# A new layout of the first stage of a trunk-layer program: two blocks of x normed together, the first FFN products by k tiles, the modulation's weights stationary

## The chip, the core and the metric

The program runs on one core of a Trainium2 chip. The metric is device time in microseconds (us) of one execution of the whole program; lower is better. An engine here is one of TensorE (PE; its weight loads are listed as PEld), VectorE (DVE), ScalarE (ACT), GpSimd (POOL) and SyncE (SP, which issues nearly all DMAs).

## What is computed

One layer of a hybrid backbone over 128 context tokens and 1024 latent tokens, width 1024, all in float32. The stage that is changed is the beginning of this:

```python
def rms_norm(x, g):
    y = x * rsqrt(mean(x * x) + EPS)
    return y * g
def adaln(cond, mod_w, mod_b):               # 9 vectors of 1024 for each of two conditions
    m = silu(cond) @ mod_w + mod_b           # mod_w is 1024 x 9216
    return m.reshape(-1, 9, 1024)
def swiglu(h, w_in, w_out):
    g, u = split(h @ w_in, 2)                # w_in is 1024 x 5632
    return (silu(g) * u) @ w_out
def trunk_layer(x, mods, ...):
    sh1, sc1, g1, sh2, sc2, g2, sh3, sc3, g3 = mods
    h = rms_norm(x, norm_ffn1) * (1 + sc1) + sh1
    x = x + 0.5 * g1 * swiglu(h, ffn1_w_in, ffn1_w_out)
    ...                                      # mixer (spatial gating MLP, latent attention), FFN 2
```

## The kernel before

**Tiling.** The 1152 tokens are three blocks of 384: block 0 holds the context and two tiles of latent tokens, blocks 1 and 2 only latent tokens. Activations lie transposed, as 8 k tiles of 128 rows (the width) by tokens. FFN 1 takes the blocks in the order 1, 2, 0 and cuts the 1152 columns into two halves of 576, and each half again into two parts (`s` 0 and 1) of 288. Every float32 operand is split into a rounded part and a remainder (`hi`, `lo`), and a product is three matmuls (`mm3`, L169).

**The products of FFN 1.** `seq` lists weight tiles by feature tile f and product number p. The products 1 and 2 of f 0 to 8 are "early": they need only the first half of the columns, p 1 the k tiles 0 to 3 and p 2 the k tiles 4 to 7. There are 18 of them, each of two parts of 12 matmuls, 432 matmuls of 288 columns in all. Their results (`ye`) go to DRAM (`ya_d`) and come back later; `ye` has three buffers, each a pair of two results, and a result with even number takes a new pair. After the early products come the units of the main loop (`units`), one for each f, of seven-product Strassen form. They need the operands of products 3, 5, 6 and 7, which are sums of parts of h; `norm_s` and `sums` (L500 to L505) make them from block 0, the last block, on DVE and ACT.

**Weights.** `make(i)` loads raw weight tiles into a ring of six (`load_parts`), copies them rounded on ACT and takes the remainder on DVE or POOL (`wi`, six buffers).

**The first stage.** `start` runs with ACT, DVE and POOL (and PE, always) in the order in which the code stands; SP is ordered by a scheduler there. It loads block 1 of x, transposes it, loads the modulation's weights for shift 1 and scale 1 (`ch` 0 and 1) in pieces of two k tiles, 1 MB each, and works out 1/rms of block 1. `mod_on_pe` multiplies with the 2-column `s2` stationary and 256 columns of weights moving (L360), copies the two rows out (L363) and transposes them back (L368); one of the eight pieces (scale 6 and 7) goes over ACT and POOL instead (`macs`, L822 and L824, and `sums`, L829). As the pieces come, x times 1/rms (`x_r`), scale and shift with the rounded copy (`h_part`) and the remainder (`l_part`) are made for block 1. Behind it, `x_block(2)` transposes block 2, `up` begins with two parts of early products, and `x_block(0)`, due 3.0 on the recording clock after the start of `up`, transposes block 0 (the clock `clk` counts estimated PE time and sets where such steps are written into the order). PSUM is taken in two layouts: four `ps_up` and four `ps_dn` banks first, then three `ps_two` pairs and two `ps_dn`.

Of the kernel before, what the change touches and what calls it, by code (L numbers as in the profile page):

```python
# [73 lines left out]
def tile_trunk(  # L74
# [15 lines left out]
    def f32(ap):  # L90
        return ap.bitcast(F32)
# [37 lines left out]
    s_ps = ps_pool("ps")  # L129
# [223 lines left out]
    def mod_on_pe(ch, k0, n, w, tp, mid=()):  # L353

        row = tp.tile([2, BW], F32, tag="modrow", name="modrow", bufs=2)
        ps = ps_dn([P, 512])
        for j in range(KT):
            if j in mid:
                mid[j]()
            nc.tensor.matmul(ps[:2, :n * P], lhsT=s2[:, j, :], rhs=w[:, j, :], start=j == 0, stop=j == KT - 1)  # L360
            clk.run(0.21 * n)

        V.tensor_copy(out=row[:, :n * P], in_=ps[:2, :n * P])  # L363

        def end():
            pt = ps_dn([P, n, 2])
            for k in range(n):
                nc.tensor.transpose(pt[:, k, :], row[:, k * P:k * P + P], ident[:2, :2])  # L368
            mod_finish(ch, k0, n, [pt[:, :, cd] for cd in range(2)])
        return end  # L370
# [25 lines left out]
    class Ffn:  # L396
# [5 lines left out]
        def __init__(self, which, order, wi, wo, early, chunks, wseq):  # L402
# [11 lines left out]
            self.ordered = None  # L414
# [160 lines left out]

        def up(self, side):

            add, mult, early, seq, hc, ys, stores = ALU.add, ALU.mult, self.early, self.seq, self.hc, {}, []
            banks = [ps_two() for _ in range(3)]
# [47 lines left out]
            for i0 in range(0, self.n_early, 6):  # L627
                for s in range(2):
                    for i in range(i0, i0 + 6):
                        f, p = seq[i]  # L630
                        self.ready(p, s)
                        ps = banks[f % 3]
                        self.product(ps, self.made[i], hc[p], p == 1, (s,))
                        if i % 2 == 0:
                            pair = self.yt.tile([P, 2, MV], F32, tag="ye", name="ye", bufs=3)
                        y = pair[:, i % 2]
                        S.activation(out=y, in_=ps[:, s, :MV], func=AF.Copy if p == 1 else AF.Silu)
                        dma(self.ya_d[f][:, p - 1, s * MV:s * MV + MV], y)
                        if s == 1:
                            self.make(i + 6)  # L640
# [120 lines left out]
    def big(name):  # L761
        return s_r.tile([P, 3 * D], F32, tag="big", name=name, bufs=3)
# [8 lines left out]
    def transpose_x(b, xn):  # L771

        st = big(f"x{b}").rearrange("p (k t) -> p k t", k=KT)
        r1 = []
        for k in range(KT + 2):
            if k < KT:
                ps = ps_dn([P, BW])
# [8 lines left out]
        dma(x_d[b], st)  # L786
# [9 lines left out]
    def start():  # L796

        m2 = [s_l.tile([P, 2 * KT * P], F32, tag="m", name="modw", bufs=2) for _ in range(2)]
        ml = s_l.tile([P, 3 * D], F32, tag="big", name="modw", bufs=1)
        mq = [F1.tile(f"q{i}", F32, (P, 4 * HT)) for i in range(4)]  # L800
        xn1 = load_x(1, big("xnat1"))
# [3 lines left out]
        sc01 = mod_in(1, 0, mq[0])  # L805
        sh01 = mod_in(0, 0, mq[2])
# [4 lines left out]
        sc67 = mod_in(1, 6, mq[1])  # L811
        sc23 = mod_in(1, 2, mq[3])
        sh23 = mod_in(0, 2, m2[0])
        sc45 = mod_in(1, 4, m2[1])
        sh67 = mod_in(0, 6, ml)
        accs = s_r.tile([P, 2, 256], F32, tag="acc", name="acc", bufs=1)

        def macs(cd):

            for j in range(KT):  # L820
                t = accs[:, cd, :] if j == 0 else t384()[:, 0:256]
                S.activation(out=t, in_=sc67[:, j, :], func=AF.Copy, scale=s2[:, j, cd:cd + 1])  # L822
                if j:
                    G.tensor_tensor(out=accs[:, cd, :], in0=accs[:, cd, :], in1=t, op=ALU.add)  # L824
# [1002 lines left out]
```

## Time and profile before

| | us |
|---|---|
| median of 3 runs | 2924.8 (2924.14 to 2924.87) |
| the profiled execution's own time | 2923.9 |
| its span, first to last instruction | 2922.1 |
| first of block 0's transposes | 61.94 |
| first product of the main loop's first unit | 139.23 |

The profile is of one execution. Lines such as L169 are lines of the kernel before; where a helper records an operation, the line is the helper's. Starts are counted from the span's beginning.

### The profile page before, as it was taken

How to read it: one execution, taken by the hardware profiler on the slowest of the kernel's cores; microseconds unless marked ns; L12 is line 12 of the kernel's file. 1: busy time of each engine (PE TensorE's matmuls, PEld its weight loads, DVE VectorE, ACT ScalarE, POOL GpSimd, SP SyncE). 2: the span in 40 equal slices, each digit the busy share in tenths (PEclk: the TensorE clock that was granted, in tenths of full speed). 3: DMA queues.
4: the chain of work that ended last, by engine and by line, in shares of the span. 5: the costliest groups of instructions: out<-in, count | busy, mean ns of one | idle time of the engine just before them, and what ended most of it. 6: DMA issues, size and time to landing. Idle time of an engine off the chain costs nothing.

```text
span 2922.1 us, 48080 instructions
## 1 busy us (share of the span) xinstructions
PE 2848.2 (97%) x19102; PEld 2812.0 (96%) x19102; DVE 1470.6 (50%) x2874; ACT 980.1 (34%) x2069; POOL 787.4 (27%) x557
## 2 busy tenths in 40 slices
PE   7899999999989999998999999999999999999997
PEld 4899999999989999998999999999999999999997
DVE  5644788888463200248447767734464422233434
ACT  5622333312042311014245555512362233331213
POOL 4156556510010011102322222223016544430000
PEclk9999999999999999999999999999999999999999
DMA  8444444666114122113621111264344422253222
GB/s 297 135 135 144 141 137 145 203 210 209 54 33 147 49 90 90 45 33 98 205 70 44 53 47 34 79 209 146 108 152 132 125 72 80 83 182 103 98 74 101
DMA packets 362453, 335.29 MB, mean 115 GB/s; under 512 B 23204, under 2 KB 320020, under 8 KB 361844
## 3 DMA queue, kind: packets, MB, share of 16 engines
q1 hardware_dynamic: 361556, 330.25, 36.3%
q8 instruction: 150, 2.46, 0.4%
q0 software_dynamic: 672, 1.97, 0.2%
q14 instruction: 75, 0.61, 0.1%
HBM read 242.59 MB, written 83.53 MB: 112 GB/s over the span
## 4 chain that ended last, share of the span: by engine, by line
PE 92%; DVE 4%; ACT 2%; issue 1%; POOL 1%; DMA 0%; SPq 0%; DVEq 0%; ACTq 0%; POOLq 0%
PE ps_two L169 37%; PE ps_up L169 19%; PE ps_dn L169 18%; PE ps_w L169 6%; PE ps_s L169 3%; PE ps_s L1404 2%; PE ps_w L204 2%; PE ps_dn L204 1%; DVE h L151 1%; PE ps_dn L1151 1%; PE ps_dn L360 1%; PE ps_b L169 0%; ACT h L150 0%; ACT q L475 0%; PE ps_dn L242 0%
## 5 line engine op out<-in xcount | busy, mean ns | idle before, releaser
L169 PE MATMUL ps_two<-h,wi 128*128 128x288 f32 x6336 | 862.7, 297 | 12.8 <-DVE wi L151 7.0
L169 PEld LDWEIGHTS ps_two<-h,wi 128*128 128x128 f32 x6336 | 850.6, 189 | 17.1 <-DVE wi L151 8.2
L151 POOL TENSOR_TENSOR wi<-raw,wi 128x512 fp32r<-128x512 f32 (+1 forms) x294 | 448.4, 1531 | 1022.2 <-ACT wi L150 896.0
L150 ACT CAST wi<-raw 128x512 fp32r<-128x512 f32 (+2 forms) x401 | 289.4, 725 | 877.3 <-PE ps_dn L169 291.7
L169 PE MATMUL ps_dn<-h,wi 128*128 128x384 f32 x2256 | 410.8, 339 | 2.6 <-DVE q L620 2.6
L169 PEld LDWEIGHTS ps_dn<-h,wi 128*128 128x128 f32 x2256 | 396.7, 189 | 2.9 <-DVE q L620 2.9
L169 PE MATMUL ps_up<-h_hi,wi 128*128 128x384 f32 x1152 | 302.1, 339 | 0.0
L169 PEld LDWEIGHTS ps_up<-h_hi,wi 128*128 128x128 f32 x1152 | 209.9, 188 | 0.0
L749 DVE SCALAR_TENSOR_TENSOR h<-ps_dn,modG,h 128x128 f32<-128x128 f32 (+2 forms) x205 | 99.3, 508 | 215.6 <-PE ps_dn L169 215.3
L385 DVE SCALAR_TENSOR_TENSOR q<-mraw,s,q 128x512 f32<-128x512 f32 x196 | 194.7, 1033 | 7.7 <-DMA mraw<-in_mod_w_dram 7.7
L169 PE MATMUL ps_up<-h_lo,wi 128*128 128x384 f32 x576 | 194.3, 337 | 0.7 <-DVE h_lo L294 0.7
L1475 POOL TENSOR_SCALAR p<-p,ast 128x1152 f32<-128x1152 f32 x64 | 79.2, 1238 | 303.4 <-PE ps_w L204 107.3
L169 PE MATMUL ps_up<-wi,h_hi 128*128 128x256 f32 (+1 forms) x864 | 160.8, 286 | 0.0
L169 PE MATMUL ps_two<-q,wi 128*128 128x288 f32 x1056 | 146.8, 294 | 0.0
L169 PEld LDWEIGHTS ps_two<-q,wi 128*128 128x128 f32 x1056 | 142.1, 188 | 0.0
L169 PE MATMUL ps_s<-kn,qn 128*128 128x384 f32 x576 | 136.9, 346 | 0.0
L150 ACT CAST pt<-ps_w 128x384 fp32r<-128x384 f32 x192 | 86.9, 488 | 145.6 <-PE ps_w L204 145.5
L169 PEld LDWEIGHTS ps_up<-wi,h_hi 128*128 128x128 f32 x864 | 133.6, 188 | 0.0
L169 PE MATMUL ps_up<-wi,h_lo 128*128 128x256 f32 (+1 forms) x432 | 122.7, 284 | 0.0
L589 ACT ACTIVATE q<-q 128x576 f32<-128x576 f32 x70 | 48.1, 687 | 219.6 <-DVE q L610 147.3
L151 DVE TENSOR_TENSOR wi<-raw,wi 128x512 fp32r<-128x512 f32 (+4 forms) x107 | 101.1, 955 | 38.9 <-ACT wi L150 38.6
L1470 DVE TENSOR_REDUCE ast<-ps_s 128x1 f32<-128x384 f32 x192 | 105.3, 553 | 26.1 <-PE ps_s L1404 24.1
(269 smaller groups left out, 4366.6 us busy)
## 6 DMA issues: line engine op xcount, KB each, us to landing
raw<-in_ffn_w_in_dram SPq DMA_DIRECT2D x212, 256.0 KB, 3.2
mraw<-in_mod_w_dram SPq DMA_DIRECT2D x112, 256.0 KB, 3.7
a_d<-q SPq DMA_DIRECT2D x88, 288.0 KB, 2.3
h<-a_d SPq DMA_DIRECT2D x32, 576.0 KB, 6.2
raw<-in_w_in_dram SPq DMA_DIRECT2D x34, 512.0 KB, 4.2
raw<-in_ffn_w_out_dram SPq DMA_DIRECT2D x32, 448.0 KB, 4.3
ya_d<-ye SPq DMA_DIRECT2D x72, 144.0 KB, 1.8
q<-ya_d SPq DMA_DIRECT2D x36, 288.0 KB, 3.9
```

The lines of the kernel that those rows point to most:

```text
L150: S.copy(out=hi, in_=src)
L151: (lo_eng or G).tensor_tensor(out=lo, in0=src, in1=f32(hi), op=ALU.subtract)
L169: nc.tensor.matmul(ps, lhsT=l[i], rhs=r[j], start=start and i == j, stop=stop and i == 1, skip_group_check=more)
L204: nc.tensor.transpose(out, in_, ident)
L360: nc.tensor.matmul(ps[:2, :n * P], lhsT=s2[:, j, :], rhs=w[:, j, :], start=j == 0, stop=j == KT - 1)
L385: V.scalar_tensor_tensor(out=ac, in0=w, scalar=s2[:, j, cd:cd + 1], in1=ac, op0=ALU.mult, op1=ALU.add)
L589: S.activation(out=y, in_=y, func=AF.Silu)
L749: V.scalar_tensor_tensor(out=xs, in0=ps[:, c0:c1], scalar=modG[:, self.which, cd, dt:dt + 1], in1=xs, op0=ALU.mult, op1=ALU.add)
L1151: nc.tensor.matmul(pm[:, i, :], lhsT=vb[b][:, i, g * P:g * P + P], rhs=wsT[:, g, :], start=True, stop=True)
L1404: nc.tensor.matmul(ps, lhsT=q2[h][:, ts_], rhs=kab[j][:, c0:c1], start=False, stop=j == 1)
L1470: V.reduce_max(out=pts[n][1][:, j:j + 1], in_=ps, axis=AX.X)
L1475: G.tensor_scalar(out=p, in0=p, scalar1=rc, scalar2=0.0, op0=ALU.mult, op1=ALU.add)
```

## The change

- All eight modulation pieces go over PE, with the 128x128 weight tile stationary and the two columns of `s2` moving, so that the result comes out transposed: 16 matmuls a piece in the program, 32 instructions on PE, since each float32 matmul is two. The copy L363, the transposes L368 and the way over ACT and POOL are gone.
- Block 1 and block 2 are both transposed and normed in `start`, with copies out of `ps_dn` and `ps_up` (now `ps_two`) in turn. PSUM has the wide layout from the beginning.
- The products of i 0 to 5 (f 0 to 2, p 1 and 2) move into `start`, part by part as the k tiles' modulation comes (`early_half`), and `up` goes on at i 6.
- The stores of x for blocks 1 and 2 stand late in `start`. SP keeps the written order there too. Block 0's transposes stay at 3.0 on the clock after the start of `up`, so now behind 14 of the 36 early parts, not behind 2.

The rest of the program stays: behind the first units, all engines have the same instructions in the same order.

```diff
-    s_ps = ps_pool("ps")
+    s_ps = ps_pool("ps", wide=True)
...
-            nc.tensor.matmul(ps[:2, :n * P], lhsT=s2[:, j, :], rhs=w[:, j, :], start=j == 0, stop=j == KT - 1)
...
+    def mod_on_pe(ch, k0, n, w):
+
+        ps = ps_dn([P, n, 2])
+        for k in range(n):
+            for j in range(KT):
+                nc.tensor.matmul(ps[:, k, :], lhsT=w[:, j, k * P:k * P + P], rhs=s2[:, j, :], start=j == 0, stop=j == KT - 1)
+        mod_finish(ch, k0, n, [ps[:, :, cd] for cd in range(2)])
...
+        def early_half(self, i, s):
+
+            f, p = self.seq[i]
+            self.ready(p, s)
+            ps = self.banks[f % 3]
+            self.product(ps, self.made[i], self.hc[p], p == 1, (s,))
+            if i % 2 == 0:
+                self.pair = self.yt.tile([P, 2, MV], F32, tag="ye", name="ye", bufs=3)
+            y = self.pair[:, i % 2]
+            S.activation(out=y, in_=ps[:, s, :MV], func=AF.Copy if p == 1 else AF.Silu)
+            dma(self.ya_d[f][:, p - 1, s * MV:s * MV + MV], y)
+            if s == 1:
+                self.make(i + 6)
...
-            for i0 in range(0, self.n_early, 6):
+            for i0 in range(self.begun, self.n_early, 6):
...
+        def m_tile():
+            return s_l.tile([P, 2 * KT * P], F32, tag="m", name="modw", bufs=3)
+        both = (ps_dn, ps_up)
+        xn1, st1, xn2, st2 = big("xnat1"), big("x1"), big("xnat2"), big("x2")
...
+        w[1, 0] = mod_in(1, 0, m_tile())
+        w[0, 0] = mod_in(0, 0, m_tile())
...
+        xn2 = load_x(2, xn2)
+        F1.load_parts(3)
+        w[1, 2] = mod_in(1, 2, m_tile())
+        w[0, 2] = mod_in(0, 2, F1.tile("q1", F32, (P, 4 * HT)))
+        w[1, 4] = mod_in(1, 4, F1.tile("q3", F32, (P, 4 * HT)))
...
+        st1, r1 = transpose_x(1, xn1, st1, both)
...
+        mod_on_pe(1, 0, 2, w[1, 0])
+        mod_on_pe(0, 0, 2, w[0, 0])
+        out1 = norm_rstd(r1)
+        r_1 = out1()
+        w[0, 4] = mod_in(0, 4, m_tile())
+        w[1, 6] = mod_in(1, 6, m_tile())
+        x_r(1, st1, r_1, 0, 0, 1, 2, 3)
+        h_part(1, 0, 0, 1)
+        l_part(1, 0, 1)
+        x_r(1, st1, r_1, 0, 4, 5, 6, 7)
+        st2, r2 = transpose_x(2, xn2, st2, both)
+        F1.take_banks()
+        for i in range(3):
+            F1.make(i, G)
+        mod_on_pe(1, 2, 2, w[1, 2])
+        out2 = norm_rstd(r2)
+        w[0, 6] = mod_in(0, 6, m_tile())
+        F1.load_parts(6)
+        xns[0] = load_x(0, big("xnat0"))
+        mod_on_pe(0, 2, 2, w[0, 2])
+        r_2 = out2()
+        h_part(1, 0, 2, 3)
+        l_part(1, 2, 3)
+        x_r(2, st2, r_2, 0, 0, 1, 2, 3)
+        h_part(2, 0, 0, 1, 2, 3)
+        l_part(2, 0, 1, 2, 3)
+        for i in range(3):
+            F1.early_half(i, 0)
+        mod_on_pe(1, 4, 2, w[1, 4])
+        x_r(2, st2, r_2, 0, 4, 5, 6, 7)
+        mod_on_pe(0, 4, 2, w[0, 4])
+        h_part(1, 0, 4, 5)
...
+        for i in range(3, 6):
+            F1.make(i, G)
+        for i in range(2):
+            F1.early_half(i, 1)
+        mod_on_pe(1, 6, 2, w[1, 6])
+        mod_on_pe(0, 6, 2, w[0, 6])
+        F1.early_half(2, 1)
+        h_part(1, 0, 6, 7)
+        l_part(1, 6, 7)
+        h_part(2, 0, 6, 7)
+        l_part(2, 6, 7)
+        dma(x_d[1], st1)
+        dma(x_d[2], st2)
+        F1.take_x(1)
+        x_r(2, st2, r_2, 1, *range(KT))
+        for s in range(2):
+            for i in range(3, 6):
+                F1.early_half(i, s)
+        h_part(2, 1, *range(KT))
+        F1.begun = 6
...
-    with tc.manual_schedule(engines={mybir.EngineType.Activation, mybir.EngineType.DVE, mybir.EngineType.Pool}):
+    with tc.manual_schedule(engines={mybir.EngineType.Activation, mybir.EngineType.DVE, mybir.EngineType.Pool, mybir.EngineType.SP}):
...
-    x_block(2)
...
-    clk.later(X_FIRST[0], lambda: x_block(0, gap=gap1))
+    clk.later(X_FIRST[0], x_block0)
```

PE at the first modulation pieces. Before, `modw` and `q` hold weights that move through the 2-column `s` (s2), with small transposes of `modrow` between:

```order
L857 MATMUL ps_up<-ident,vec 128x112
L360 MATMUL ps_dn<-q_169,s_114 2x256 x2
L368 MATMUL ps_dn<-ident,modrow 128x2 x2
L360 MATMUL ps_dn<-q_169,s_114 2x256 x6
L360 MATMUL ps_dn<-q_170,s_114 2x256
L204 MATMUL ps_dn<-ident,st 128x128 x3
```

And in the changed program, where `s` moves through the weights:

```order
L204 MATMUL ps_two<-ident,xnat_164 128x128 x3
L846 MATMUL ps_two<-ident,vec 128x112
L358 MATMUL ps_dn<-s_114,modw 128x2 x32
L242 MATMUL ps_dn<-ones,r_221 128x1
L242 MATMUL ps_dn<-ones,r_228 128x1
```

Two whole pieces now stand in one run ahead of block 1's sums of squares (`r`), and `vec` (the gains and mod_b) ahead of both. The counts are those of the program: PE executes each float32 matmul as two instructions.

SP at the stores of x (`x_d_72` is block 1, `x_d_73` block 2, `x_d_71` block 0; `ya_d_137` to `139` are the early results of f 0 to 2). Before:

```order
L88 DMA raw<-in_ffn_w_in_dram 128x4x128 x2
L88 DMA x_d_73<-x_540 128x3072
L88 DMA ya_d_137<-ye 128x288
L88 DMA ya_d_138<-ye 128x288
L88 DMA x_d_71<-x_638 128x3072
L88 DMA ya_d_139<-ye 128x288
```

And now:

```order
L88 DMA raw<-in_ffn_w_in_dram 128x4x128
L88 DMA x_d_72<-x_165 128x3072
L88 DMA x_d_73<-x_167 128x3072
L88 DMA ya_d_137<-ye 128x288
L88 DMA ya_d_138<-ye 128x288
L88 DMA ya_d_139<-ye 128x288
```

Two stores of x, 1.5 MB each, now stand one behind the other ahead of the results of the parts (3,0), (4,0) and (5,0).

ACT at block 0's transposes (`x_638` before, `x_892` now; `t` are squares). Before:

```order
L225 ACTIVATE t_594<-x_540 128x384
L225 ACTIVATE t_597<-x_540 128x384
L225 ACTIVATE t_600<-x_540 128x384
L637 ACTIVATE ye<-ps_two 128x288 x2
L783 COPY x_638<-ps_dn 128x384
L222 ACTIVATE r_654<-x_638 128x384
```

And now (`q_747` and `q_748` are the second half of block 2):

```order
L579 ACTIVATE ye<-ps_two 128x288
L150 CAST wi<-raw 128x512
L834 ACTIVATE q_747<-q_747,modT,modA 128x192 x4
L834 ACTIVATE q_748<-q_748,modT,modA 128x192 x4
L579 ACTIVATE ye<-ps_two 128x288 x2
L782 COPY x_892<-ps_dn 128x384
L222 ACTIVATE r_908<-x_892 128x384
```

Block 0's copies followed block 2's squares; now eight scale-and-shifts of block 2's second half stand between a weight tile of the early products and them.

## Rows read from the trace of the kernel before

**Rows 1.** The page of the profile: the engines' busy time (part 1), TensorE's busy tenths in 40 slices of 73 us (part 2), the chain that ended last by engine (part 4).

```profile
PE 2848.2 (97%) x19102; PEld 2812.0 (96%) x19102; DVE 1470.6 (50%) x2874; ACT 980.1 (34%) x2069; POOL 787.4 (27%) x557
...
PE   7899999999989999998999999999999999999997
...
PE 92%; DVE 4%; ACT 2%; issue 1%; POOL 1%; DMA 0%; SPq 0%; DVEq 0%; ACTq 0%; POOLq 0%
```

**Rows 2.** Windows of 10 us. Columns: the window, its length, busy us (and instructions) of PE, PEld, DVE, ACT and POOL, the granted TensorE clock, the DMA engines' share, GB/s moved.

```profile
10.00:20.00 10.00, 8.99 (x48) 5.32 (x48) 6.78 (x20) 4.30 (x11) 3.19 (x3) 1.00 1.10 342
...
50.00:60.00 10.00, 6.46 (x33) 5.42 (x32) 6.46 (x11) 7.74 (x18) 7.19 (x6) 0.66 0.67 212
...
70.00:80.00 10.00, 7.15 (x51) 6.25 (x49) 6.62 (x32) 4.95 (x14) 0.00 (x0) 0.99 0.32 119
...
100.00:110.00 10.00, 8.58 (x63) 8.11 (x62) 10.00 (x16) 10.00 (x24) 0.00 (x0) 1.00 0.24 79
110.00:120.00 10.00, 6.59 (x43) 6.36 (x42) 10.00 (x16) 8.51 (x18) 0.00 (x0) 0.87 0.30 95
```

**Rows 3.** The timeline of PE. Columns: start in us, length in us, engine, line, operation, out<-in, shapes, count, and idle time before it with its releaser. The first row is the beginning of block 0's transposes, the second begins the first unit of the main loop (four products of 24, in one run), the third the second unit.

```profile
61.94 0.81 PE L204 MATMUL ps_dn<-ident,xnat 128*128 128x128 f32 x6
...
139.23 12.95 PE L169 MATMUL ps_two<-h,wi 128*128 128x288 f32 x96 [0.50 <-ACT ye L637]
...
155.19 12.86 PE L169 MATMUL ps_two<-h,wi 128*128 128x288 f32 x96
```

**Rows 4.** The same timeline of PE, the steps whose prices are used: block 1's transposes (L204), modulation products (L360), the sums of squares (L242), the spreading of 1/rms (L204 of st), the end of block 0's transposes.

```profile
7.43 4.76 PE L204 MATMUL ps_dn<-ident,xnat 128*128 128x128 f32 x22 [1.17 <-DMA xnat<-in_x_sample_dram]
12.13 2.32 PE L360 MATMUL ps_dn<-q,s 128*2 128x256 f32 x10
...
22.98 0.54 PE L204 MATMUL ps_dn<-ident,st 128*128 128x128 f32 x3
...
27.94 3.62 PE L360 MATMUL ps_dn<-modw,s 128*2 128x256 f32 x16
...
65.31 1.03 PE L204 MATMUL ps_dn<-ident,xnat 128*128 128x128 f32 x6 [0.17 <-ACT x L783]
...
67.78 1.39 PE L242 MATMUL ps_dn<-ones,r 128*128 128x1 f32 x12
```

**Rows 5.** The timeline of DVE, ACT and POOL in the first 90 us, the same columns: first and last step of a 1/rms (L247, L213), the copy of its spread (L256), x times it (L865), scale and shift and rounded copy of one k tile (two L840 with the copy L842 between them), remainder (L847), rounded copies of weights (L150), a product's result (L637), the first copy and the last addition of block 0's transposing (L783, L226), eight scale-and-shifts of 192 columns (L475).

```profile
17.15 0.16 DVE L247 TENSOR_SCALAR st<-ps_dn 128x3 f32<-128x3 f32 x1 [1.37 <-PE ps_dn L242]
...
19.11 0.16 DVE L213 SCALAR_TENSOR_TENSOR st<-st 128x3 f32<-128x3 f32 x1
...
23.56 0.48 ACT L256 COPY t<-ps_dn 128x384 f32<-128x384 f32 x1 [9.23 <-PE ps_dn L204]
...
27.32 1.94 DVE L865 TENSOR_TENSOR q<-x,t 128x384 f32<-128x384 f32 x4
...
27.89 0.71 ACT L840 ACTIVATE q<-q,modT,modA 128x384 f32<-128x384 f32 x1 [3.85 <-DVE q L865]
...
29.05 0.70 ACT L840 ACTIVATE q<-q,modT,modA 128x384 f32<-128x384 f32 x1
29.19 0.54 DVE L847 TENSOR_TENSOR h<-q,h 128x384 fp32r<-128x384 f32 x1
...
48.41 2.18 ACT L150 CAST wi<-raw 128x512 fp32r<-128x512 f32 x4
...
60.53 0.41 ACT L637 ACTIVATE ye<-ps_two 128x288 f32<-128x288 f32 x1 [0.31 <-PE ps_two L169]
...
62.46 0.48 ACT L783 COPY x<-ps_dn 128x384 f32<-128x384 f32 x1
...
67.85 1.10 DVE L226 TENSOR_TENSOR r<-r,t 128x384 f32<-128x384 f32 x1 [0.17 <-ACT t L225]
...
82.22 3.62 ACT L475 ACTIVATE q<-q,modT,modA 128x192 f32<-128x192 f32 x8
```

**Rows 6.** The timeline of block 0's norm and of the first unit's weights: the copy of the spread 1/rms, the last four remainders of block 0's operands (DVE), then the first and the last step of the first unit's weights.

```profile
87.00 0.48 ACT L256 COPY t<-ps_dn 128x384 f32<-128x384 f32 x1 [0.37 <-PE ps_dn L204]
...
117.80 2.75 DVE L151 TENSOR_TENSOR q<-q,q 128x576 fp32r<-128x576 f32 x4
...
127.48 0.69 DVE L558 TENSOR_TENSOR s<-raw 128x512 f32<-128x512 f32 x1 [3.91 <-DMA raw<-in_ffn_w_in_dram]
...
131.88 1.29 POOL L151 TENSOR_TENSOR wi<-raw,wi 128x512 fp32r<-128x512 f32 x1 [63.34 <-ACT wi L150]
```

**Rows 7.** DMA issues of the first 140 us. Columns: out<-in, queue, operation, count, KB of one, median us from issue to landing.

```profile
ya_d<-ye SPq DMA_DIRECT2D x36, 144.0 KB, 1.8
x_d<-x SPq DMA_DIRECT2D x3, 1536.0 KB, 6.6
```

**Rows 8.** The clock: windows of 2 us of PE alone (length, busy us and count, granted clock, DMA share, GB/s); the weight loads at 117.94 us; and the transposes of block 1, once before 11.5 us and once after 11.7 us (duration of one in ns, min/median/max).

```profile
52.00:54.00 2.00, 0.00 (x0) 0.65 0.63 164
...
118.00:120.00 2.00, 2.00 (x8) 0.50 0.38 108
...
117.94 2.90 PEld L169 LDWEIGHTS ps_two<-h,wi 128*128 128x128 f32 x12 [3.64 <-DVE wi L151]
...
L204 PE MATMUL ps_dn<-ident,xnat x16: 421/421/473, 7.9 to 11.3; 128*128 128x128 f32 x16
...
L204 PE MATMUL ps_dn<-ident,xnat x5: 272/273/421, 11.3 to 11.9; 128*128 128x128 f32 x5
```

More of the change, by code (lines that the diff above doesn't have):

```diff
@@ L626, in up @@
                 self.make(i, V)
-            for i0 in range(0, self.n_early, 6):
+            for i0 in range(self.begun, self.n_early, 6):
                 for s in range(2):
                     for i in range(i0, i0 + 6):
[L630 to L640, printed above, removed]
+                        self.early_half(i, s)
             self.ready(6, 0)
@@ L761, in big @@
     def big(name):
[L762 removed]
+        return s_r.tile([P, 3 * D], F32, tag="big", name=name, bufs=4)
     def load_x(b, xn):
@@ L810, in start @@
         dma(vec[40:112, :], mod_b[0].rearrange("(k p) -> k p", p=P))
[L811 to L824, printed above, removed]
@@ L826, in sums @@
-        def sums(cd):
-            ps = ps_dn([P, 2])
-            for k in range(2):
-                nc.tensor.matmul(ps[:, k:k + 1], lhsT=accs[:, cd, k * P:k * P + P], rhs=ones[:, 0:1], start=True, stop=True)
-            mod_finish(1, 6, 2, [ps], (cd,))
-        def x_h(k):
-            return F1.xq[k // 4, 0][:, k % 4, 0:BW]
-        def hl(k):
-            return (z[:, k % 4, 0:BW] for z in F1.hc[1 + k // 4])
-        def h_part(*ks):
+        xn2 = load_x(2, xn2)
+        F1.load_parts(3)
@@ L839, in h_part, with pieces, x_r @@
+        w[1, 2] = mod_in(1, 2, m_tile())
+        w[0, 2] = mod_in(0, 2, F1.tile("q1", F32, (P, 4 * HT)))
+        w[1, 4] = mod_in(1, 4, F1.tile("q3", F32, (P, 4 * HT)))
+        F1.operands(1, 2)
+        F1.take_x(0)
+        def pieces(b):
+            return [(t, hs, bs) for t, hs, bs in F1.cuts(b) if t == 0]
+        def x_r(b, st, r, t0, *ks):
             for k in ks:
-                S.activation(out=x_h(k), in_=x_h(k), func=AF.Identity, scale=modA[:, 0, 1, k:k + 1], bias=modT[:, 1, 0, k:k + 1])
@@ L841, in h_part @@
-                hi, lo = hl(k)
-                S.copy(out=hi, in_=x_h(k))
-        def l_part(*ks):
+                for t, hs, bs in F1.cuts(b):
+                    if t == t0:
+                        V.tensor_tensor(out=F1.xq[k // 4, t][:, k % 4, hs], in0=st[:, k, bs], in1=r[:, bs], op=ALU.mult)
+        def h_part(b, t0, *ks):
             for k in ks:
-                hi, lo = hl(k)
-                V.tensor_tensor(out=lo, in0=x_h(k), in1=f32(hi), op=ALU.subtract)
-        outs = []
-        st1, r1 = transpose_x(1, xn1)
@@ L851, in start @@
-        sh45 = mod_in(0, 4, big("modw"))
-        F1.load_parts(6)
-        xns[2] = load_x(2, big("xnat2"))
-        F1.operands(1, 2)
-        fin = mod_on_pe(1, 0, 2, sc01, s_r, {5: lambda: outs.append(norm_rstd(r1))})
+                for t, hs, bs in F1.cuts(b):
+                    if t == t0:
+                        xs = F1.xq[k // 4, t][:, k % 4, hs]
+                        S.activation(out=xs, in_=xs, func=AF.Identity, scale=modA[:, 0, 1, k:k + 1], bias=modT[:, 1, 0, k:k + 1])
+                        if t == 0:
+                            S.copy(out=F1.hc[1 + k // 4][0][:, k % 4, hs], in_=xs)
@@ L856, in start, with l_part @@
+        def l_part(b, *ks):
+            for k in ks:
+                for t, hs, bs in pieces(b):
+                    hi, lo = (z[:, k % 4, hs] for z in F1.hc[1 + k // 4])
+                    V.tensor_tensor(out=lo, in0=F1.xq[k // 4, 0][:, k % 4, hs], in1=f32(hi), op=ALU.subtract)
+        st1, r1 = transpose_x(1, xn1, st1, both)
         ps = ps_up([P, P])
```

82 lines of the change are left out of this document (19 added, 63 removed).

## The prediction

> **What bounds the kernel now.** First the page: PE is busy for 97% of the span, its tenths are below 9 in the first two of 40 slices, 146 us, and seldom later, and the chain that ended last is 92% PE [rows 1]. So nearly everywhere time can only be won by fewer matmuls; the change keeps the main matmuls, and can win only what PE waits or idles in those two slices. The windows show where that is: PE is busy for 6.46 of 10 us at 50 to 60, 7.15 at 70 to 80, 6.59 at 110 to 120 [rows 2]. Next, the place from which both programs are alike: the first unit begins at 139.23 us, the second at 155.19 us [rows 3], and from there PE runs dense. 15.96 us for 120 matmuls is 0.133 us each. **The time therefore moves by as much as the first unit's beginning moves.** Of the 139.2 us before it, the 432 early matmuls need 57.5 us; the other 82 us are what is at stake. The last thing to see is who is late ahead of the first unit: DVE is busy for 10.00 of 10 us from 100 to 120, ACT for 10.00 and 8.51 [rows 2], with the norm of block 0. That work starts with block 0's transposes, at 61.94 us [rows 3], behind 2 of the 36 early parts.
>
> **The first products come earlier.** I follow the changed order step by step; all durations are of before.
> - Block 1's transposes end at 12.2 us as before (7.43 + 4.76) [rows 4]. The third tile of x has landed by 7.43 us; then the two modulation pieces, 2.1 MB at 342 GB/s [rows 2], take 6.1 us, and `vec`, which is queued behind them and now stands ahead of the first piece on PE, lands at 13.5 us; with its transpose, 13.8.
> - A modulation matmul with 128 weight columns and 2 moving ones isn't in the trace. The nearest row is the sum of squares, 128 weight columns and 1 moving one: 12 in 1.39 us, 0.116 each [rows 4]. A piece is 32 of them, 3.7 us; before it was 16 in 3.62 to 3.7 us [rows 4] and small transposes. So on PE the new form saves nearly nothing; what goes is the copying back, which PE mostly didn't wait for. Two pieces: 21.2 us.
> - Sums of squares 1.4, the 1/rms 2.1 (17.15 to 19.27), spread and copy 1.1 (22.98 to 24.04) [rows 4, 5]: 25.8 us. ACT then makes two k tiles of block 1, 1.16 each (27.89 to 29.05), behind the first x times 1/rms, 0.5; DVE is taken until 30.7 by eight of those (1.94 for 4) and two remainders [rows 5]. Block 2's transposes need both engines: from the first copy to the last transpose they took 3.9 us for block 0 (62.46 to 66.34), and 6.5 to the last addition (68.95) [rows 4, 5]. From about 30.3: 34.5 and 36.6 us.
> - Piece 3.7, sums of squares 1.4, piece 3.7 (the 1/rms lies beside it), spread 0.5: 43.9 us. The copy 0.5, two more k tiles 2.3, a remainder 0.5 and the last matmuls 0.4 end the first part at 47.6; two more parts, 1.6 each: 50.8. Two pieces 7.4, two parts 3.2, two pieces 7.4, one part 1.6: 70.4 us.
> - Block 1's k tiles 6 and 7: on ACT a result 0.41, a weight tile 0.55 (2.18 for 4), two k tiles 2.3, then a remainder 0.5 and the hand-overs: the part (3,0) ends at 74.8, the next five at 82.8 us.
>
> **A new wait.** The part (3,1) has an odd number, so its result takes the half pair that (5,0) has used, and ACT must wait until (5,0)'s store has landed. A store of a result lands in 1.8 us, one of x in 6.6 [rows 7]. Two of x now stand ahead, issued at about 73: 6.6 + 4.6 (1.57 MB at 342 GB/s) + 1.3 for the three results gives 85.5. Behind the waiting ACT are two results, three weight tiles, block 2's second half and the copies of block 0; PE waits for the bank of (3,1) until 86, 3.2 us.
>
> **Block 0's chain.** Two parts later, at 89.2, PE comes to block 0's transposes. ACT has then to do three results, three weight tiles, eight scale-and-shifts (3.6) and two results, 7.2 us from 85.5, so the first copy is at 92.7, and the transposes end at 96.6. Three parts 4.8, sums 1.4, three parts 4.8, spread 0.5, the copy behind a result and a weight tile 1.1: 109.2. From that copy's end to the last of block 0's remainders before: 87.48 to 120.55, 33.1 us [rows 6], with the same weight remainders between, and DVE full from 100 on [rows 2]. It can't shrink: 142.3. DVE now also makes three of the first unit's sums among the last remainders, 0.69 each [rows 6], one remainder comes behind: 143.7; before they were made later and waited for a DMA, with PE still on early parts. Rounded copy 0.7: 144.4; POOL's remainder 1.29 [rows 6], hidden by one matmul: 145.6. PE alone would be ready at 96.6 + 22 parts of 1.6 + 1.9 = 133.7. It idles, and the clock falls after such an idle (granted 0.65 at 52 to 54, with no matmul in 52 to 54; 0.50 at 118 to 120, after 3.64 us of waiting) [rows 8]: at the low level of 1.2 GHz a product matmul took 2.90 / 12 = 0.242 us, 1.83 times 0.133, about 1 us lost in the first ten. **Sum: 146.6 against 139.2, 7.4 us later.** Against the profiled execution that is 2923.9 + 7.4 = 2931.3; the median is 0.9 above that execution, so 2932.2, rounded 2932, 0.25% slower. What hid block 0's chain before was 34 early parts, 54 us of PE; now 22 parts, 35 us, lie beside it, and the 12 that went ahead wait for the modulation.
>
> **The unknown price.** Whether matmuls of two columns keep PE's clock at 2.4 GHz no row shows: the narrow run of before is 1.4 us long [rows 4], the new ones 7.4. Ends: they cost 0.116 at either level, or 1.83 times as much, 0.212. I take 0.116 at the high level, since the sums of squares are the nearest row, and keep the other end.
> Block 1's transposes bear on it: the same instruction took 421 ns up to 11.3 us and 272 after that [rows 8], though PE had done nothing but transposes. The Trainium skill (TensorE: Matmul & The Clock Gate, Part 4: PE-mode transpose) says that transposes don't count as PE-busy in the same way and don't bring the full clock. By that rule block 2's transposes and the narrow pieces around them would leave the clock low up to the first products, as in the first rival, 2954; by the trace's row they can raise it, and the sum stays at 2932.
>
> **Rivals.**
> - *The narrow pieces let the clock fall.* The clock fell when PE did little in a stretch (0.65 at 52 to 54), and in a narrow run nearly no columns move. Then six of the eight pieces run at 1.2 GHz: 6 x 32 x 0.096 = 18.4 us; the parts behind them start slow, some 35 matmuls at +0.109, 4 us. All lie ahead of block 0's transposes, so all count: 2932 + 22 = 2954. If the weight loads don't slow, only the parts do: 2936. For it: it is one long stretch with hardly a column; against it: PE is never without an instruction.
> - *Not slower: the stores don't stand in the way.* Place: the wait of (3,1). If the stores of x drain before 79 us (issued earlier than 73, or in parallel with the results), ACT never stops: minus 3.2 on PE and minus 3.5 at block 0's copies, which then come as PE does. The first unit begins at 139.9, 2925.5 us, no change. Decides: the store of (5,0) landing by 80 us. For it: results of before land in 1.8 us; against it: one queue issues them all.
> - *Faster.* PE alone would be ready at 133.7, or 127.0 without that wait and the late copies: 2919.3, or 2912.6. It needs block 0's chain some 11 us shorter, against a DVE that is full for 20 us in both [rows 2].
>
> **How the numbers follow.** My forecast, 2932 within 2927 to 2936 (some dozen hand-overs between engines, a few tenths each, are in none of its rows), gets 0.44; the falling clock 0.40, from 2936 to 2957; the stores out of the way 0.11, 2922 to 2927; faster 0.05. 2925 to 2957 leaves out about 0.1 below and less than 0.1 above. A measurement here can tell 0.2%, 5.85 us, from no change: the limit is 2930.65. Of the forecast's own 0.44, a little over 0.6 lies above it. Slower: 0.27 + 0.40 = 0.67; same: 0.17 + 0.10 = 0.27; faster: 0.05 + 0.01 = 0.06.
>
> **What would show it.** Right: first product at 43 to 45 us, an ACT wait on a DMA of `ya_d` near 80, block 0's first transposes near 89, DVE full from about 109 to 143, PE idle just ahead of the first unit at about 144. The clock: narrow rows at 0.116 with the granted clock at 1.00 for me, at 0.2 with 0.50 for the rival. Wrong: block 0's transposes by 82 us, or DVE done with block 0 before PE has finished the early parts; then the sum's last term, the chain, wasn't the limit.

## The result, and the profile after

The changed kernel takes **2957.3 us** (median of 4 runs, 2955.54 to 2961.63) against 2924.8 before: ratio 1.0114, 95% interval 1.0096 to 1.0131, slower by 1.1% or 32.5 us. That is near the time of the prediction's first rival (2954, "the narrow pieces let the clock fall"), not of its forecast (2932), and 0.3 us above the range. The profiled execution is the slowest of the four, 2961.6 us with a span of 2959.9, so distances read from its timeline can be some us more than those of medians.

First the windows, of PE alone this time (length, busy us and count, granted clock, DMA share, GB/s):

```profile
16.00:36.00 20.00, 17.69 (x84) 0.50 1.08 345
40.00:66.00 26.00, 25.30 (x109) 0.50 0.32 112
67.00:70.00 3.00, 3.00 (x29) 1.00 0.40 128
72.00:84.00 12.00, 12.00 (x55) 0.51 0.00 1
88.00:104.00 16.00, 15.29 (x64) 0.50 0.40 136
```

Before, the clock was low only for a few us behind a wait [rows 2, 8]. Now it is at 0.50, the lower level, in most of the first 104 us, although PE is busy for 25.30 of 26 us and for 12.00 of 12. Near 15 and 39 us it fell beside waits of PE, of 2.35 us and of 1.59 and 1.35; near 70 and 87 us it fell within narrow runs in which PE never paused. Next PE's timeline of the same stretch: the modulation pieces (L358, 32 matmuls each, two pieces in the rows of 64), the first product, some products, the beginning of block 0's transposes, and the first unit.

```profile
14.88 13.25 PE L358 MATMUL ps_dn<-s,modw 128*128 128x2 f32 x64
...
41.33 6.99 PE L358 MATMUL ps_dn<-s,modw 128*128 128x2 f32 x32
...
50.73 6.97 PE L358 MATMUL ps_dn<-s,q 128*128 128x2 f32 x32
...
58.09 1.79 PE L169 MATMUL ps_two<-h,wi 128*128 128x288 f32 x6
60.16 7.59 PE L169 MATMUL ps_two<-h,wi 128*128 128x288 f32 x30 [0.27 <-ACT h L836]
67.58 4.54 PE L358 MATMUL ps_dn<-s,q 128*128 128x2 f32 x32
71.99 6.97 PE L358 MATMUL ps_dn<-s,modw 128*128 128x2 f32 x32
78.81 5.63 PE L169 MATMUL ps_two<-h,wi 128*128 128x288 f32 x24
84.28 11.03 PE L358 MATMUL ps_dn<-s,modw 128*128 128x2 f32 x64
...
116.06 0.82 PE L204 MATMUL ps_dn<-ident,xnat 128*128 128x128 f32 x6
...
168.59 0.85 PE L169 MATMUL ps_two<-h,wi 128*128 128x288 f32 x2 [7.13 <-ACT wi L150]
```

A two-column matmul takes 6.97 / 32 = 0.218 us where the clock is low, and the eight pieces together 49.8 us, not the 29.6 that I summed. The first product comes at 58.09 us; the sum said 43.9. Block 0's transposes come at 116.06 (89.2), the first unit at 168.59 (146.6), against 61.94 and 139.23 before [rows 3]. DVE is full ahead of the unit, as forecast (the window of 10 us, columns as in [rows 2]):

```profile
140.00:150.00 10.00, 10.00 (x78) 10.00 (x77) 10.00 (x17) 9.94 (x23) 0.00 (x0) 1.00 0.65 194
```

Last, two waits that stand later: ACT's, for the store of a result, and PE's at the first small transposes of the down products. For this one the row of before follows in its own fence, with the 192 matmuls behind it.

```profile
112.29 0.41 ACT L579 ACTIVATE ye<-ps_two 128x288 f32<-128x288 f32 x1 [4.96 <-DMA ya_d<-ye]
...
615.40 0.63 PE L204 MATMUL ps_dn<-ident,mraw 128*128 128x128 f32 x4 [2.84 <-DVE q L629]
```

```profile
580.32 0.66 PE L204 MATMUL ps_dn<-ident,mraw 128*128 128x128 f32 x4 [1.13 <-POOL mraw L934]
580.74 34.16 PE L169 MATMUL ps_dn<-h,wi 128*128 128x384 f32 x192
```

### The profile page after: what moved, and what is told of

It is laid out like the page before. It is cut to its first block, busy times and chain, and to the rows that moved or that the text cites. A ratio compares the mean times of both kernels' runs of the same rounds, so it can differ in the third digit from the quotient of the medians.

```text
span 2959.9 us, 48263 instructions
## 1 busy us (share of the span) xinstructions
PE 2880.7 (97%) x19224; PEld 2863.8 (97%) x19224; DVE 1469.4 (50%) x2867; ACT 973.0 (33%) x2053; POOL 774.5 (26%) x543
## 4 chain that ended last, share of the span: by engine, by line
PE 92%; DVE 3%; ACT 2%; issue 2%; DMA 1%; SPq 0%; POOL 0%; DVEq 0%; ACTq 0%; POOLq 0%
PE ps_two L169 37%; PE ps_up L169 19%; PE ps_dn L169 18%; PE ps_w L169 6%; PE ps_s L169 3%; PE ps_s L1410 2%; PE ps_w L204 2%; PE ps_dn L358 2%; PE ps_dn L204 1%; PE ps_dn L1157 1%; PE ps_b L169 0%; ACT h L150 0%; PE ps_dn L242 0%; ACT q L465 0%; SPq L88 0%
## 5 line engine op out<-in xcount | busy, mean ns | idle before, releaser
L150 ACT CAST wi<-raw 128x512 fp32r<-128x512 f32 (+2 forms) x401 | 289.0, 725 | 881.0 <-PE ps_dn L169 294.5
L150 ACT CAST pt<-ps_w 128x384 fp32r<-128x384 f32 x192 | 87.0, 489 | 145.5 <-PE ps_w L204 145.5
```

The source lines that it names most:

```text
L150: S.copy(out=hi, in_=src)
```

## The experiments

**Order and form apart.** The theory: matmuls with two moving columns let the clock fall, whatever the order. The rival: the new order itself, with its waits. Two kernels cross them: the new order with the old form of the pieces, and the old order with the new form.

```
     (new order)
-    nc.tensor.matmul(ps[:, k, :], lhsT=w[:, j, k * P:k * P + P], rhs=s2[:, j, :], ...)
+    nc.tensor.matmul(ps[:2, :n * P], lhsT=s2[:, j, :], rhs=w[:, j, :], ...)
+    V.tensor_copy(out=row, in_=ps[:2, :n * P]); two transposes back
     (old order: the reverse, no copy, no transposes back)
```

> The new order kept word for word, but the modulation pieces in the form of before: s2 stationary, 256 columns moving, the row copied back by VectorE and transposed by two small matmuls. Theory (in the two-column form PE's clock falls): the granted clock stays at 1.00 from 12 us to the first products, a piece takes 3.7 us and about 1 us for copying back, the first product comes at 44 to 49 us (58.1 after), block 0's first transposes at 88 to 96 (116.1 after), the first unit at 142 to 150 (168.6 after), the time is 2929 to 2936 us. Rival (the order itself keeps PE slow or late, whatever the form): the clock is low in the same stretches, block 0's transposes come after 108 us and the time stays within 2950 to 2962.

> The kernel before with the new form of the modulation pieces alone (weights stationary, two columns moving, no copying back), its order as it was. Theory (the form lets the clock fall, whatever the order): the granted clock is 0.50 in the narrow stretches, a piece takes about 7 us in place of 3.6, the first product comes 10 to 25 us after 58.0, and since block 0's chain from its transposes to the first unit needs 53 to 55 us and before had 77, part of that is hidden: 2933 to 2945 us. Rival (the order is what lets the clock fall): pieces at 3.7 us, 2921 to 2927 us.

New order, old form: 2945.05 us, ratio 1.0061 [1.0046, 1.0076]. Old order, new form: 2937.65 us, ratio 1.0040 [1.0025, 1.0055]. The new form alone costs the old order 11.2 us (2937.65 - 2926.42, the kernel before in the same session); seven of the eight pieces have it there, one still goes over ACT and POOL. PE's timeline of this second kernel and two windows of it:

```profile
12.83 2.55 PE L360 MATMUL ps_dn<-s,q 128*128 128x2 f32 x20
...
47.64 15.50 PE L360 MATMUL ps_dn<-s,modw 128*128 128x2 f32 x72
```

```profile
10.00:15.00 5.00, 5.00 (x32) 1.00 1.10 331
...
45.00:50.00 5.00, 5.00 (x26) 0.50 0.18 44
```

The pieces begin at 1.00, with 0.13 us a matmul; the clock falls while they run, and then they take 0.215. The first kernel missed its 2929 to 2936: of its pieces five ran at 1.00 for the most part (3.61 us where a piece ran in one), but PE now waited for DVE's copy of the row behind seven of the eight, 0.5 to 2.3 us each time. Of its timeline, the longest of these waits and the beginning of block 0's transposes:

```profile
76.81 0.28 PE L367 MATMUL ps_dn<-ident,modrow 2*128 2x2 f32 x2 [2.29 <-DVE modrow L362]
...
101.75 0.82 PE L204 MATMUL ps_dn<-ident,xnat 128*128 128x128 f32 x6
```

So it doesn't price the clock alone.

**The price at both levels.** Is it the clock, or is a weight load dear by itself? Behind every second two-column matmul a 256-column one is put that nobody reads. It writes into the piece's bank, and the modulation sums come out otherwise; the time is that of the same instructions.

```
+                if j % 2:
+                    nc.tensor.matmul(whole[:, 128:384], lhsT=ident, rhs=w[:, j, :], ...)
```

> The changed kernel with work added that nobody reads: behind each second two-column matmul a matmul of 256 columns into unused columns of the same bank, 64 more in all, about 0.45 us each at the high clock by the old form's 3.62 us for 16 halves, 28.6 us of PE. Theory (the clock, not the weight loads themselves, makes the form dear): granted clock 1.00 in the pieces from the second on, two-column matmuls at 0.11 to 0.12 us between the fillers, a piece about 7.2 us as in the changed kernel, but transposes, sums and first products at their high price: 2949 to 2957 us, not slower than the changed kernel in spite of 64 more matmuls. Rival (a 128-column weight load is dear by itself, about 0.21 us at either level): a piece takes 10.3 us, 2975 to 2985 us.

It took 2988.51 us, ratio 1.0209 [1.0192, 1.0227], outside what either side expected: from 14 us until the first products, which begin at 86 us, the clock never came up, and each piece took some 13.6 us, 8 x 1.70. The theory's forecast of the time fell; the rows still decide on the price. Two windows and PE's timeline, a group of two-column matmuls and fillers in each:

```profile
55.00:85.00 30.00, 29.98 (x110) 0.50 0.28 97
95.00:115.00 20.00, 20.00 (x140) 1.00 0.15 44
```

```profile
16.72 0.85 PE L359 MATMUL ps_dn<-s,modw 128*128 128x2 f32 x4
17.43 1.20 PE L361 MATMUL ps_dn<-modw,ident 128*128 128x256 f32 x2
18.42 0.85 PE L359 MATMUL ps_dn<-s,modw 128*128 128x2 f32 x4
...
94.57 0.50 PE L359 MATMUL ps_dn<-s,q 128*128 128x2 f32 x4
...
95.45 0.50 PE L359 MATMUL ps_dn<-s,q 128*128 128x2 f32 x4
```

The same group repeats every 18.42 - 16.72 = 1.70 us at 0.50 and every 95.45 - 94.57 = 0.88 us at 1.00. A weight load isn't dear by itself; the rival falls. What I had not expected: the mixture doesn't bring the clock up (0.50 from 55 to 85 us with PE busy for 29.98 of 30), but once the first products have raised it, the same mixture keeps it.

**The columns alone.** Now only the number of moving columns changes, with the changed kernel's order and its 256 matmul instructions; the sums are read from one column of each 64.

```
-        ps = ps_dn([P, n, 2])
+        ps = ps_dn([P, n, 2, 64])
-    rhs=s2[:, j, :]
+    rhs=s2[:, j, :].unsqueeze(2).to_broadcast([P, 2, 64])
```

> The changed kernel with one thing altered: each of the 256 modulation matmuls moves 128 columns in place of 2 (the two columns of s2, each repeated 64 times by a stride of zero), with the same weights in the same order; the sums are read from two of the columns. Theory (two-column matmuls let the clock fall, the weight loads are not dear by themselves): at the high level a piece takes 3.4 to 3.8 us although 64 times as many columns move, since a 128-column weight load and 128 moving columns take about the same (transposes of before: 0.11 each at granted 1.00), the clock stays at or comes back to 1.00 within a piece, block 0's first transposes come at 92 to 100 us (116.1 after, 101.8 with the old form), the time is 2932 to 2943 us. Rival (PE's waits in the new order keep the clock low, not the number of columns): the pieces run at granted 0.50 as before, 7 us each, 2954 to 2962 us.

> The kernel before, its order as it was, with the modulation pieces weights-stationary and 128 columns moving. Theory (the number of moving columns is all that the stationary form costs): the clock stays at 1.00 from 12 to 50 us, a piece takes 3.4 to 3.8 us, the time is that of before within 2 us, some 11 us less than with two columns moving. Rival (the stationary form costs by itself, by its weight loads or by the banks that it holds longer): 2933 to 2940 us as with two columns.

New order: 2934.96 us, ratio 1.0030 [1.0020, 1.0040]. Old order: 2925.51 us, 0.9995 [0.9986, 1.0005], as before. PE's timeline of the first (the last row begins the second unit), then two windows of it, columns as above:

```profile
14.98 9.01 PE L358 MATMUL ps_dn<-s,modw 128*128 128x128 f32 x64
...
46.72 1.04 PE L169 MATMUL ps_two<-h,wi 128*128 128x288 f32 x6
...
53.99 3.73 PE L358 MATMUL ps_dn<-s,q 128*128 128x128 f32 x32
...
90.70 0.82 PE L204 MATMUL ps_dn<-ident,xnat 128*128 128x128 f32 x6
...
142.80 0.85 PE L169 MATMUL ps_two<-h,wi 128*128 128x288 f32 x2 [7.13 <-ACT wi L150]
...
162.31 12.86 PE L169 MATMUL ps_two<-h,wi 128*128 128x288 f32 x96
```

```profile
35.00:40.00 5.00, 4.98 (x22) 0.51 0.85 225
55.00:60.00 5.00, 5.00 (x47) 1.00 0.63 193
```

With 64 times the columns a piece takes 3.73 us in place of 6.97, block 0's transposes come 25.4 us sooner, the first unit 25.8 us sooner, and the median falls by 22.4 us. The clock still falls beside PE's waits of 2.31 and 1.42 us at block 2's transposes (0.51 from 35 to 40 us), but now it comes back within a piece. In either order the narrow columns are what the form costs: all of the 11.2 us in the old, 22 to 24 of the 32.5 in the new (24 if each kernel is set against the kernel before of its own session, which measured 2926.3 here).

**The new wait and block 0's chain.** The prediction gave 3.2 us on PE to ACT's wait for the store of (5,0), and 3.5 at block 0's copies. In the kernel with the old form the pairs of result tiles are taken by the count of results, which removes it.

```
-            if i % 2 == 0:
+            if self.n_y % 2 == 0:   # n_y counts the results made
```

> As the kernel with the new order and the old form, and each new pair of result tiles is taken by the count of results made, not by the part's number, so that (3,1) no longer writes into the half that (5,0) has just used. Theory of the prediction's new wait and of the chain (ACT waits some 5 us for a store behind two stores of x, and block 0's copies and all behind them wait with it): ScalarE's wait on a DMA of ya_d ahead of the eight scale-and-shifts is gone, block 0's first copy and the first unit come 3 to 6.5 us earlier than in the kernel with the old form alone, and the time is 3 to 6.5 us less than its. Rival (block 0's chain isn't what ends last there, or the wait moves to the next pair): within 1 us of it.

2944.76 us against 2945.05: no difference, as its rival said. The wait of ACT was gone, but the first unit came only 1.5 us sooner, 152.50 against 154.00. Then, on the wide form and with the pairs by count, block 0 is brought on sooner, in two ways:

```
-X_FIRST = {0: 3.0}
+X_FIRST = {0: 0.4}
-        F1.norm_start(0, r1, st, gap=gap1)
+        F1.norm_start(0, r1, st, gap=gap1, first=1.2, wait=4)
     (the other: transpose_x(0, ...) in start(), ahead of the pieces (1,6) and (0,6),
      and the stores of x behind the results of the sixth part)
```

> 128 columns moving in the new order, result pairs by count, and block 0 brought on sooner: its transposes stand one quarter of a part behind the six early parts of the first stage in place of two parts, its sums 1.2 and the spread of its 1/rms about 2 us of PE's work behind in place of 3.6 and 3. Theory (the end is set by block 0's chain, so what shortens the chain or starts it sooner moves the first unit by as much): from block 0's first transposes to the first unit 43 to 48 us in place of 51 to 53, the first unit 8 to 12 us and the time 7 to 12 us earlier than in the kernel with 128 columns alone. Rival (PE's own work or the first unit's weights end last): within 2 us of it.

> 128 columns moving, result pairs by count, and block 0's transposes and squares stand ahead of the last two modulation pieces, where ScalarE idles, its sums between these, the spread behind the part that follows; x is stored behind the results of the sixth part. Theory (block 0's chain): the chain then begins some 15 to 20 us sooner and runs beside 30 early parts in place of 22, so that PE's own work ends last: the first unit at 128 to 138 us, the time 2913 to 2924 us, below both kernels. Rival (what is won in the chain is lost on PE, which now waits for ScalarE and VectorE among the first six parts): first unit after 140 us, 2926 us or more.

The first took 2929.44 us, 5.5 less than with wide columns alone; the first unit came at 138.38, 4.4 sooner. The chain from the transposes to the unit stayed at 51.7 us (86.70 to 138.38; 52.1 with wide columns alone) in place of the 43 to 48 expected: PE now waited 3.8 us for ACT between the transposes, before 2.5, so the spread of 1/rms came only 1.7 us sooner behind them, and 1.3 of that was lost behind it. The second took 2942.81 us, ratio 1.0055 [1.0040, 1.0070], more than the first and than wide columns alone. Its waits of PE between the first product and the first unit, then one of ACT's:

```profile
PE ps_two L169 <- ACT ye L580: 6.0, 3, 3.0
PE ps_dn L204 <- ACT x L783: 4.2, 1, 4.2
PE ps_two L169 <- DVE wi L151: 3.0, 1, 3.0
```

```profile
ACT h L150 <- DMA x_d<-x: 4.7, 2, 4.2
```

Block 0's chain no longer ends last (the first unit, at 154.22, waits 0.5 us for a result of the early products), but PE waits for ACT at the transposes and, with ACT standing still for the stores of x, later for its results: with three smaller kinds 17.4 us of waits in all. Its rival was right.

**PE's waits ahead of the first products.** The rest of the order's price is searched there, on the first of these two kernels.

```
-        transpose of vec; mod_on_pe(1, 0, 2, w[1, 0])
+        mod_on_pe(1, 0, 2, w[1, 0], vec_t)     # vec's transpose behind the matmuls
         out1 = norm_rstd(r1)
+        st2, r2 = transpose_x(2, xn2, st2, both)
         r_1 = out1()
```

> The kernel with 128 columns moving, pairs by count and the sooner block 0, and in addition PE's waits ahead of the first products filled: the transpose of the norm vectors stands behind the first modulation piece's matmuls in place of ahead of them, and block 2's transposes stand right behind block 1's sums of squares, where PE waited 2.3 us for the 1/rms and 1.4 us for ScalarE. Theory (what the order lost beside the narrow columns are these waits and the low clock that follows each, 9.0 us for two pieces in place of 7.1, 5.8 for one in place of 3.6, 0.64 for three transposes in place of 0.32; all stands ahead of block 0's chain): first product at 35 to 40 us in place of 46.7, block 0's transposes and the first unit 5 to 10 us earlier, 2919 to 2925 us, below the kernel before (which measured 2926.3 here). Rival (the loads of weights and x set the beginning): first product after 44 us, 2927 to 2930 us.

> As the one with the filled waits, and block 0's transposes brought into the first stage again, now between the last two modulation pieces (so that ScalarE is done with the k tiles when PE comes to them), its sums behind the third part, the spread behind the fourth; the stores of x[1] and x[2] stand behind the first three results and that of x[0] right behind its transposes, so that no later tile waits for them. Theory (in the kernel with early block 0 it was PE's waits, 20 us in all, and the store of x that ate the gain): PE waits less than 8 us between the first product and the first unit, the first unit at 122 to 132 us, 2909 to 2922 us. Rival (ScalarE and VectorE together are the bound of the stage, so that PE waits elsewhere): first unit after 132 us, 2922 us or more.

2927.72 us and 2928.24 us, ratios 1.0002 [0.9993, 1.0011] and 1.0008 [0.9999, 1.0017]: as before, not below it. In the first, the pieces begin at 12.45 us at the high clock and the waits named are gone, but a new one of 6.90 us stands ahead of the piece (0,2), and the first product comes at 44.14, not 35 to 40: the numbers of its rival. Still the first unit begins at 135.14 us, 4.1 sooner than in the kernel before. In the second, with block 0's transposes in the first stage again, it begins only at 141.56 (122 to 132 expected): between the first product and the unit PE waits 10.8 us in all for ACT and DVE, and its rival was right too. That the 4.1 us of the first are lost again by the end led to the next place: PE's wait near 580 us.

> As the kernel with the filled waits, and block 1's and 2's transposes begin with a bank of the large tiles in place of one of the small ones, so that the accumulators of the first stage take the same banks as in the kernel before. In the changed kernel, and in all with its first stage, PE waits 2.8 to 3.0 us for VectorE at the first small transposes of the down products, near 575 us of the filled-waits kernel, and runs on at the low clock, where the kernel before waited 1.1 us. Theory (these transposes take the bank of the last accumulator that VectorE reads out, because the tiles of the first stage were taken in another order): the wait is 1.1 us or less there, the whole 3 to 4.5 us less than that kernel's 2927.7, 2923 to 2925 us. Rival (VectorE is late there for other reasons, such as the time at which weights land): still 2.5 us or more, 2926 to 2929 us.

```
-        both = (ps_dn, ps_up)
+        both = (ps_up, ps_dn)
```

The rows of PE, of the kernel with filled waits and, in its own fence, of this one:

```profile
579.20 1.09 PE L204 MATMUL ps_dn<-ident,mraw 128*128 128x128 f32 x4 [3.01 <-DVE q L631]
579.94 35.96 PE L169 MATMUL ps_dn<-h,wi 128*128 128x384 f32 x192
```

```profile
133.72 0.53 PE L169 MATMUL ps_two<-h,wi 128*128 128x288 f32 x2 [1.55 <-ACT wi L150]
...
575.89 0.66 PE L204 MATMUL ps_dn<-ident,mraw 128*128 128x128 f32 x4 [1.12 <-POOL mraw L947]
576.31 34.17 PE L169 MATMUL ps_dn<-h,wi 128*128 128x384 f32 x192
```

**2920.75 us, ratio 0.9982 [0.9973, 0.9991]: below both kernels.** With the accumulators' order of before, the wait is 1.12 us again, as before, and the 192 matmuls behind it no longer begin at the low clock (34.17 us in place of 35.96; 34.16 in the kernel before). In the two profiled executions wait and slow matmuls make 3.7 us, and the first unit begins 1.4 us sooner. The medians differ by 7.0, more than that and more than the 3 to 4.5 expected; where the rest lies is not shown.

The last kernel tests whether shared transfers are behind the wait ahead of the piece (0,2):

```
-        w[1, 4] = mod_in(1, 4, F1.tile("q3", ...))            # at the start
+        w[1, 4] = mod_in(1, 4, big("modw"))                   # behind block 2's transposes
```

> As the kernel with the banks as before, and the load of the piece (1,4) goes to the place of block 2's x, which comes free with block 2's transposes, so that it and the two loads behind it are issued some 8 to 12 us later and don't share the transfer rate with the piece (0,2), for which PE waited 6.9 us in the kernel with the filled waits. Theory (the loads share the rate, 345 to 350 GB/s from 20 to 35 us, so what is issued sooner lands no sooner and holds up what is needed next): the wait ahead of that piece falls below 2 us, the first product comes at 36 to 40 us in place of 44.1, the first unit 4 to 7 us earlier, 2917 to 2921 us. Rival (the order of landing doesn't follow the order of issue, or ScalarE isn't ready with the first k tiles): first product after 42 us, within 2 us of the kernel with the banks as before.

2923.16 us, 0.9985 [0.9977, 0.9994], no better; the wait is unchanged, 5.97 us in both, and the first product at 43.40. But the edit hardly moved the load of (1,4). Its issue (length in ns, three times, then its start in us, twice) and the time to its landing, in the kernel with the banks as before and then in this one:

```profile
L88 SPq DMA_DIRECT2D q<-in_mod_w_dram x1: 1545/1545/1545, 19.6 to 19.6; - x1
DMA to landing us min/median/max: 11.6/11.6/11.6
...
L88 SPq DMA_DIRECT2D modw<-in_mod_w_dram x1: 1468/1468/1468, 20.0 to 20.0; - x1
DMA to landing us min/median/max: 11.4/11.4/11.4
```

It landed at 31.2 us and then at 31.4, not 8 to 12 later, so this run doesn't test the theory. The first trace speaks against it all the same: the weights of (0,2) were issued ahead of these, at 16.4 us on the same queue, and PE went on 5.9 us after these had landed. The profile names no releaser for the wait. PE's, DVE's and POOL's rows in the kernel with the banks as before give a reading:

```profile
37.12 5.64 PE L358 MATMUL ps_dn<-s,q 128*128 128x128 f32 x32 [5.97 <-issue]
```

```profile
28.02 1.95 DVE L828 TENSOR_TENSOR q<-x,t 128x384 f32<-128x384 f32 x4
...
31.52 5.16 DVE L828 TENSOR_TENSOR q<-x,t 128x384 f32<-128x384 f32 x4
36.60 0.15 DVE L342 TENSOR_TENSOR modT<-ps_dn,vecT 128x2 f32<-128x2 f32 x1
```

```profile
31.61 4.66 POOL L151 TENSOR_TENSOR wi<-raw,wi 128x512 fp32r<-128x512 f32 x3 [3.93 <-ACT wi L150]
```

PE goes on at 37.12, just behind DVE's reading (36.60 to 37.01) of the piece (1,2), whose bank the piece (0,2) takes next. That reading stands behind four multiplications that take 5.16 us beside POOL's remainders, 1.95 without. This was read, not tried by a run of its own.

## Why the prediction was wrong, step by step

- **The step that failed** is in "The unknown price": "I take 0.116 at the high level, since the sums of squares are the nearest row". The row was 1.4 us long and ran between wide work. In long runs the two-column matmul costs 0.218, the other end of the bound, 0.212. My reason against the rival, "PE is never without an instruction", was no reason: PE was busy for 12.00 of 12 us at 0.51. The Trainium skill (TensorE: Matmul & The Clock Gate, Part 1, HAM oscillation) puts a fallen clock down to gaps in which PE stands idle; near 70 us it fell, and to 84 us it stayed low, without one, and the measurement decides. The rule on transposes that the prediction weighed gave the same time as the rival, but transposes are not the cause: with 128 columns the same transposes stand in the same places and the time is 2934.96 us, and in the kernel with filled waits block 2's run at the high level, three in 0.33 us.
- **The first rival** had the mechanism and nearly the size: 18.4 us in the pieces, 4 in the products, 22 in all. Measured: pieces 49.8 us against 33.4 with 128 columns, 16.4; block 0's transposes 25.4 us later, so the other 9 us lie mostly in products and sums of squares at the low level (the latter 2.70 us each against 1.40); the first unit 25.8 us later, the median 22 to 24. The sum of 146.6 us plus 22 gives the first unit at 168.6; it came at 168.59. That the two agree is luck: with 128 columns the unit begins at 142.80, 3.8 us before the sum, and the narrow columns cost it 3.8 us more than 22.
- **The forecast's own sum comes out where the clock comes back.** It said 7.4 us later. With 128 columns the second unit begins at 162.31 us, before at 155.19 [rows 3]: 7.1 us. Within it errors cancel, so this is in part luck: the first product came 2.8 us later than summed, block 0's transposes 1.5, the chain from there to the unit took 52.1 us, not 57.4, and the first unit, begun at the low clock, took 19.5 us to the second, before 16.0, where the sum had about 1 for that. In the working, 30.3 plus 3.9 and 6.5 are 34.2 and 36.8, not 34.5 and 36.6, which decides nothing.
- **The new wait** was there, 4.96 us of ACT, but cost PE 1.1 us where I had 3.2. In the kernel with the old form, taking it away brought the unit 1.5 us sooner, where the sum had 6.7 with block 0's copies, and the whole no sooner.
- **"The time therefore moves by as much as the first unit's beginning moves"** is short by some 3 us: the order in which the accumulators' banks are first taken reaches to PE's wait that stood at 580 us before and adds 1.7 us of wait (2.84 for 1.13) and 1.2 in slow matmuls behind it (35.34 for 34.16). The kernel with 128 columns waits 2.9 us there too. I had looked at no row behind the first units.
- **"On PE the new form saves nearly nothing"** was read from the old order, where the copying back is hidden. In the new order the old form costs 2945.05 us against 2934.96 with 128 columns.
- Right as forecast in kind: DVE full with block 0's chain, PE idle just ahead of the unit (7.13 us, where the sum had some 12), and the products' slow start behind it.

## What to carry to other kernels

Busy isn't enough for PE's clock: before a product is turned round so that its weights are stationary and only a few columns move, look at how long such a run lasts, and price a long one at the lower level, as the runs of 7 us and more were paid here; repeating the columns by a stride of zero cost nothing here and gave back 22 to 24 us. When a stage is laid out anew, read the timeline also far behind it, since the order in which accumulator tiles are first taken decided a wait 440 us later. And a step brought forward is worth what the engine that serves it has free at the new place: block 0's transposes, moved up, cost PE more waits than the chain had.

## What the runs showed of the hardware that was not expected

- A matmul instruction with a 128 x 128 weight load and 128 moving columns takes 0.117 us (3.73 / 32) at granted 1.00; with two moving columns it takes 0.13 at 1.00 and 0.215 to 0.218 at 0.50. At the high level 128 columns cost no more than two.
- A mixture of two-column and 256-column matmuls ran from 55 to 85 us at 0.50 with PE busy for 29.98 of 30 us and didn't raise the clock; behind products that had raised it, the clock stayed at 1.00 from 95 to 115 us, of which all but 3.5 us of products is that mixture.
- DVE's multiplications of two 128 x 384 operands took 0.49 us each alone and 1.29 beside POOL's remainders. The Trainium skill (SBUF — State Buffer, SBUF: two separate sides) says that a DVE operation with two SBUF inputs and a POOL operation exclude each other on a shared port; the trace nearly agrees: four multiplications and three remainders took 5.16 us together, and one behind the other they would take 1.95 + 3 x 1.29 [rows 6], 5.8 us.
